# A two-layer decoder trunk on one core: output weights of the last stage split once and kept in DRAM, the scan's carry and the first loads moved to other queues, norm roots as one power, and u kept

## The chip, the cores and the metric

The kernel runs on one core of a Trainium2 chip. The metric is device time in microseconds (us) of one execution, here the median of three runs. Besides the runs one execution was recorded by the hardware profiler; every row of the profile comes from that one.

The engines are named as in the profile: PE is TensorE's matmul, PEld its weight load, DVE VectorE, ACT ScalarE, POOL GpSimd, SP SyncE. SP, ACT and POOL also issue DMAs (SPq, ACTq, POOLq); each of them works through its own queue in order.

## What is computed

x has 2048 rows of 1024. Layer 0 mixes with an mLSTM, layer 1 with an RG-LRU, and a norm ends the trunk:

```python
for layer in range(2):
    u = rmsnorm(x, ln_g[layer])
    y = mlstm_mixer(u, ...) if layer == 0 else rglru_mixer(u, ...)
    x = x + y
return rmsnorm(x, final_g)

def rglru_mixer(u, ...):
    xr, g = split(u @ w_in)                  # 1024 -> 2 x 1536
    xc = causal_dwconv(xr, conv_w, conv_b)   # 4 taps
    r, ig = sigmoid(xc @ w_a + b_a), sigmoid(xc @ w_x + b_x)   # 8 diagonal blocks of 192
    log_a = -8.0 * r * softplus(-lam)
    bt = sqrt(-expm1(2 * log_a)) * (ig * xc)
    h[t] = exp(log_a)[t] * h[t-1] + bt[t]    # scan along the sequence
    return (h * silu(g)) @ w_out             # 1536 -> 1024
```

`rmsnorm` multiplies by the inverse root of the mean square, so each norm needs one root per row of x.

## The kernel before, in words

Activations lie with features on the 128 partitions and time along the free dimension, in blocks of TB = 512 columns, four blocks in all. Each fp32 product is made of three: both operands are split into a high part (a cast, ACT, line 735) and a low part (source minus high part, DVE, line 738), and `mm3` (lines 360 to 364) adds hh, hl and lh in PSUM.

There are four phases, one after the other:

- **a1** (line 385): layer 0's input projections. Two blocks of 512 columns are taken together as the halves of a Strassen-like product (class `Slab`, lines 39 to 286): `u11`, `u21` are parts of the first block's u, `t1` to `t4` and `u22` are combinations of both blocks (`combos`, line 196). It runs for s = 0 and s = 1. `early` (line 230) makes products that need the first block alone while the second block's norm is made (`stat` and `norm`, lines 607 to 611). Weight combinations `s1` to `s4` are split for s = 0, stored to DRAM from POOL's queue (line 90) and loaded by SP for s = 1 (line 95).
- **a2** (line 749): the mLSTM recurrence.
- **b1** (line 1042): layer 0's output projection and layer 1's input projection, the latter again in Strassen-like form.
- **b2** (line 1218): the last stage, that is gates, scan, output projection and the final norm. A step list (lines 1227 to 1234) takes, for each of four blocks, eight gate items ("g", 21 matmuls each) and 24 output items ("r", 12 matmuls each): one g, then three r that belong to five g earlier.

*Norm roots.* `stats_sum` (line 1019) sums squares on PE (`ssum`), DVE scales the sum into `stx` (line 1027), and `rsqrt` (line 334) makes the inverse root `rc` on DVE: a shift, a subtraction and three Newton steps of three, eleven instructions of 128 x 4. Then PE spreads `rc` over the partitions (`rows`, line 140; `srow`, line 1034). It is called twelve times: four times each in a1, b1 and b2.

*u of the first block.* `combos` needs u of the first block in one piece. `backs` (line 187) rebuilds it from high and low parts in eight DVE additions, into tiles of t1 and t4; u of the second block goes to eight tiles `x`, which have eight buffers.

*Weights in b2.* `fetch` (line 1237) brings the next weights; `weights` keeps up to three items ready ahead in high priority. A gate item's raw weights (128 x 896, one buffer) are split in block 0, high and low parts are stored to `d_gw` by POOL (line 1252) and loaded again by SP in blocks 1 to 3 (line 1244), each in one of two buffers. An output item's raw weights (128 x 512, three buffers) are loaded and split in each of the four blocks (lines 1247 and 1249), into one of four buffers.

*First xc.* `load(0, 0)` brings the first three xc tiles by DMAs from ACT's queue (line 1279); all others come from SP's (line 1282).

*Carry.* After each group's three scans (line 1318) POOL copies the last column to `hcarry` (line 1320), which the same group's scan in the next block starts from.

*Order.* The order of instructions in each engine's queue is planned when the kernel is built, from dependences, priorities and planned times; `tc.high_priority()` moves what stands in it ahead.

Of the kernel before, what the change touches and what calls it, by code (L numbers as in the profile page):

```python
# [7 lines left out]
F32 = mybir.dt.float32  # L8
# [30 lines left out]
class Slab:  # L39
# [156 lines left out]
    def combos(self, U, xs, rc, fs, row=None):  # L196
# [7 lines left out]
        us = xs if row is not None else [self.x() for _ in range(KD)]  # L204
# [10 lines left out]
        for j in range(4):  # L215
            U["u22", j] = self.operand("u22", j, us[j + 4], "v")
            v.tensor_tensor(us[j + 4], f2[j], f1[j], op=ALU.subtract)
# [71 lines left out]
class Trunk:  # L289
    def __init__(self, ctx, tc, vecs, gbias):  # L290
# [14 lines left out]
        nc.vector.memset(self.one1, 1.0)  # L305
        self.lc = cp.tile([P, 48], F32, name="lc")
# [27 lines left out]
    def rsqrt(self, pool, out, x, w, rows=P):  # L334
        nc = self.nc
        b = pool.tile([P, w], I32, tag="rsb", name="rsb")
        t = pool.tile([P, w], F32, tag="rst", name="rst")
        nc.vector.tensor_scalar(b[:rows], x.bitcast(I32), 1, None, op0=ALU.logical_shift_right)
        nc.vector.tensor_scalar(out.bitcast(I32), b[:rows], -1.0, float(0x5F3759DF), op0=ALU.mult, op1=ALU.add)
        for _ in range(3):  # L340
            nc.vector.tensor_tensor(t[:rows], out, out, op=ALU.mult)
            nc.vector.scalar_tensor_tensor(t[:rows], t[:rows], -0.5, x, op0=ALU.mult, op1=ALU.mult)
            nc.vector.scalar_tensor_tensor(out, t[:rows], 1.5, out, op0=ALU.add, op1=ALU.mult)

    def stats(self, pool, psp, acc, rc, rb, tag="st"):

        nc = self.nc
        ps = psp.tile([P, 512], F32, tag=tag, name=tag)
        for c in range(4):
            nc.tensor.matmul(ps[:, c:c + 1], acc[:, c * P:(c + 1) * P], self.ones, start=True, stop=True)  # L350
        x = pool.tile([P, 4], F32, tag="stx", name="stx")
        nc.vector.tensor_scalar(x, ps[:, 0:4], 1.0 / DM, EPS, op0=ALU.mult, op1=ALU.add)
        self.rsqrt(pool, rc, x, 4)
        pb = psp.tile([P, 512], F32, tag=tag, name=tag)
        for c in range(4):
            nc.tensor.matmul(pb[:, c * P:(c + 1) * P], rc[:, c:c + 1].to_broadcast([P, P]), self.ident,
                             start=True, stop=True)
        nc.scalar.copy(rb, pb)
# [1139 lines left out]
```

## Time and profile before

| | us |
|---|---|
| median of 3 runs | 3058.34 |
| lowest, highest | 3058.22, 3059.42 |
| profiled execution, its time | 3061.18 |
| profiled execution, its span | 3059.1 |
| mean granted TensorE clock | 0.983 |

The phases lie in the span about as follows: a1 from 0 to 1010 us, a2 to 1710, b1 to 2565, b2 to the end.

| us of the span | PE busy, us | DVE busy | ACT busy | granted clock | DMA share |
|---|---|---|---|---|---|
| 40 to 400 (a1) | 347.9 | 258.1 | 169.6 | 0.98 | 0.67 |
| 1020 to 1700 (a2) | 658.9 | 555.1 | 430.0 | 0.98 | 0.45 |
| 1715 to 2095 (b1) | 372.2 | 235.4 | 114.8 | 1.00 | 0.62 |
| 2340 to 2560 (b1) | 220.0 | 132.1 | 69.0 | 1.00 | 0.62 |
| 2560 to 2600 (b2) | 28.1 | 13.9 | 22.6 | 0.79 | 0.82 |
| 2680 to 2790 (b2) | 105.9 | 86.1 | 78.4 | 0.99 | 0.63 |

A row of a timeline reads: start, duration, engine, line of the kernel, operation, what is written and read, shape, count; in brackets how long the engine had been idle and what ended that. The DMA share is the mean busy share of the core's 16 DMA engines.

### The profile page before, as it was taken

To read this page: it belongs to the slowest core of one execution; us is meant where nothing else is said; L and a number is where in the kernel's file an instruction comes from. 1 tells how busy PE (TensorE), PEld (TensorE's weight loads), DVE (VectorE), ACT (ScalarE), POOL (GpSimd) and SP (SyncE) were. 2 spreads that over 40 slices of the span, in tenths; PEclk is the share of its full clock that TensorE was granted. 3 is DMA by queue.
4 is the path that set the end of the run, shared out by engine and by line. 5 is a ranking of instruction groups with operands and counts; after the bars stand their busy time and mean duration, and the time that the engine had idled before them with its cause. 6 is when DMAs were issued, how large, how long until landed. Compare 5 with 4: busy or idle time off the path is not lost. (4 is left out here: it accounts for less than half of the span.)

```text
span 3059.1 us, 43718 instructions
## 1 busy us (share of the span) xinstructions
PE 2927.9 (96%) x15730; PEld 2506.7 (82%) x15730; DVE 2153.6 (70%) x3774; ACT 1509.3 (49%) x2514; POOL 211.7 (7%) x394
## 2 busy tenths in 40 slices
PE   6999999999999999999999899999999998899997
PEld 4799987899988898989999777877888886687786
DVE  7866789534566688888888555687778374887775
ACT  5444545323344566666666322333445234876772
POOL 0111110000000011111111000000110000110100
PEclk9999999999999999999999999999999998999999
DMA  6766677666777645454443665566666656656643
GB/s 218 255 216 231 230 249 241 204 202 206 222 222 228 193 129 167 128 171 132 148 144 102 200 192 176 182 210 216 217 216 224 206 188 230 240 183 236 237 134 128
DMA packets 308985, 600.63 MB, mean 196 GB/s; under 512 B 27808, under 2 KB 106400, under 8 KB 308768
## 3 DMA queue, kind: packets, MB, share of 16 engines
q1 hardware_dynamic: 222784, 389.79, 41.4%
q10 hardware_dynamic: 59184, 107.77, 10.0%
q0 software_dynamic: 26800, 100.28, 8.5%
q8 instruction: 124, 2.03, 0.3%
q14 instruction: 93, 0.76, 0.1%
HBM read 388.86 MB, written 208.86 MB: 195 GB/s over the span
## 5 line engine op out<-in xcount | busy, mean ns | idle before, releaser
L735 ACT CAST s<-raw 128x512 fp32r<-128x512 f32 (+1 forms) x360 | 222.3, 621 | 497.8 <-PE acc L364 195.4
L738 DVE TENSOR_TENSOR s<-raw,s 128x512 fp32r<-128x512 f32 (+1 forms) x360 | 246.9, 689 | 90.4 <-ACT s L735 84.9
L362 PE MATMUL acc<-yh,s 128*128 128x512 f32 x512 | 202.3, 398 | 10.1 <-ACT yh L735 3.4
L363 PE MATMUL acc<-yl,s 128*128 128x512 f32 x512 | 202.8, 396 | 0.0
L364 PE MATMUL acc<-yh,s 128*128 128x512 f32 x512 | 202.2, 395 | 0.0
L362 PE MATMUL acc<-yh,wh 128*128 128x512 f32 x384 | 150.4, 399 | 14.3 <-ACT yh L735 9.4
L363 PE MATMUL acc<-yl,wh 128*128 128x512 f32 x384 | 153.5, 401 | 0.3 <-DVE yl L738 0.2
L364 PE MATMUL acc<-yh,wl 128*128 128x512 f32 x384 | 152.1, 399 | 1.1 <-DVE wl L738 1.0
L662 DVE SCALAR_TENSOR_TENSOR xc<-xm,vec,xc 128x512 f32<-128x512 f32 x192 | 140.5, 748 | 14.3 <-ACT xc L660 13.4
L735 ACT CAST s<-sum 128x512 fp32r<-128x512 f32 (+1 forms) x120 | 74.3, 620 | 146.4 <-PE pa L364 43.6
L362 PEld LDWEIGHTS acc<-yh,s 128*128 128x128 f32 x512 | 96.6, 189 | 35.5 <-ACT yh L735 3.8
L735 ACT CAST wh<-wr 128x512 fp32r<-128x512 f32 (+1 forms) x104 | 65.4, 641 | 107.8 <-PE acc L363 76.1
L364 PEld LDWEIGHTS acc<-yh,s 128*128 128x128 f32 x512 | 96.8, 189 | 22.7
L363 PEld LDWEIGHTS acc<-yl,s 128*128 128x128 f32 x512 | 96.8, 189 | 22.4 <-DVE yl L738 0.4
L930 DVE SCALAR_TENSOR_TENSOR C<-C,dl,kv 128x516 f32<-128x516 f32 x112 | 83.7, 747 | 44.6 <-PE kv L364 44.5
L738 DVE TENSOR_TENSOR wl<-wr,wh 128x512 fp32r<-128x512 f32 (+1 forms) x104 | 73.5, 717 | 56.2 <-ACT wh L735 50.9
L362 PE MATMUL gate<-xch,wh 128*128 128x512 f32 x224 | 91.9, 411 | 19.2 <-ACT xch L735 9.3
L738 DVE TENSOR_TENSOR s<-sum,s 128x512 fp32r<-128x512 f32 (+1 forms) x120 | 82.6, 689 | 39.3 <-ACT s L735 38.0
L662 DVE SCALAR_TENSOR_TENSOR xc<-xr,vec,xc 128x512 f32<-128x512 f32 x144 | 104.9, 747 | 7.3 <-ACT xc L660 6.3
L735 ACT CAST Ch<-C 128x516 fp32r<-128x516 f32 x120 | 74.8, 623 | 64.9 <-DVE da L948 48.2
L362 PE MATMUL pj<-vwh,xmh 128*128 128x512 f32 x256 | 103.3, 403 | 0.0
L364 PE MATMUL pj<-vwh,xml 128*128 128x512 f32 x256 | 100.4, 392 | 0.0
(418 smaller groups left out, 9615.2 us busy)
## 6 DMA issues: line engine op xcount, KB each, us to landing
d_wx<-s POOLq DMA_DIRECT2D x64, 512.0 KB, 4.0
s<-d_wx SPq DMA_DIRECT2D x64, 512.0 KB, 4.4
raw<-in_wout_dram SPq DMA_DIRECT2D x128, 256.0 KB, 3.1
raw<-in_wxz_dram SPq DMA_DIRECT2D x124, 256.0 KB, 4.4
d_wr<-s POOLq DMA_DIRECT2D x48, 512.0 KB, 3.5
s<-d_wr SPq DMA_DIRECT2D x48, 512.0 KB, 4.6
wr<-in_rwout_dram SPq DMA_DIRECT2D x96, 256.0 KB, 2.9
raw<-in_rwin_dram SPq DMA_DIRECT2D x84, 256.0 KB, 3.9
```

Of the source, the lines that this page charges most:

```text
L362: mm(out, sh, mh, start=first, stop=False, skip_group_check=resumed)
L363: mm(out, sh, ml, start=False, stop=False, skip_group_check=resumed)
L364: mm(out, sl, mh, start=False, stop=last, skip_group_check=resumed)
L662: nc.vector.scalar_tensor_tensor(out, x[:, j:j + TB], self.v(wn, m * 4 + j), out, op0=ALU.mult, op1=ALU.add)
L735: a = nc.scalar.copy(hi, src)
L738: b = (nc.gpsimd if lo_eng == "p" else nc.vector).tensor_tensor(lo, src, hi.bitcast(F32), op=ALU.subtract)
L930: nc.vector.scalar_tensor_tensor(C2, C2, self.dl[:, r:r + 1], p2, op0=ALU.mult, op1=ALU.add)
```

## The change

- `rsqrt` becomes one POOL instruction, a power with exponents from a tile of -0.5, in all twelve places.
- In a1 `combos` gets `held`: `backs` is not called; the scaled x tiles of the first block are passed as u, and u of the second block goes to tiles of t1 and t4.
- In b2 high and low parts lie side by side in one tile `both`. Output weights are split in block 0 alone, stored by POOL to a new DRAM tile `ow`, and loaded by SP in blocks 1 to 3 in one DMA of 512 KB. Gate weights are stored and loaded in one DMA in place of two.
- The first three xc are loaded from POOL's queue.
- The carry is copied by ACT.
- `stats`, which nothing calls, is gone.

```diff
-    def combos(self, U, xs, rc, fs, row=None):
+    def combos(self, U, xs, rc, fs, row=None, held=False):
...
-        us = xs if row is not None else [self.x() for _ in range(KD)]
+        if held:
+            us = [self.temp("t4", "l", j) for j in range(4)] + [self.temp("t1", "h", j) for j in range(4)]
+        else:
+            us = xs if row is not None else [self.x() for _ in range(KD)]
...
             U["u22", j] = self.operand("u22", j, us[j + 4], "v")
+            if held:
+                us[j + 4] = f2[j]
             v.tensor_tensor(us[j + 4], f2[j], f1[j], op=ALU.subtract)
...
+        self.mhalf = cp.tile([P, 4], F32, name="mhalf")
+        nc.vector.memset(self.mhalf, -0.5)
...
-    def rsqrt(self, pool, out, x, w, rows=P):
-        nc = self.nc
-        b = pool.tile([P, w], I32, tag="rsb", name="rsb")
-        t = pool.tile([P, w], F32, tag="rst", name="rst")
-        nc.vector.tensor_scalar(b[:rows], x.bitcast(I32), 1, None, op0=ALU.logical_shift_right)
-        nc.vector.tensor_scalar(out.bitcast(I32), b[:rows], -1.0, float(0x5F3759DF), op0=ALU.mult, op1=ALU.add)
-        for _ in range(3):
-            nc.vector.tensor_tensor(t[:rows], out, out, op=ALU.mult)
-            nc.vector.scalar_tensor_tensor(t[:rows], t[:rows], -0.5, x, op0=ALU.mult, op1=ALU.mult)
-            nc.vector.scalar_tensor_tensor(out, t[:rows], 1.5, out, op0=ALU.add, op1=ALU.mult)
...
+    def rsqrt(self, out, x, w):
+        self.nc.gpsimd.tensor_tensor(out, x, self.mhalf[:, 0:w], op=ALU.pow)
...
-                    t[:] = [S.invrms(acc1), S.backs(U)]
+                    t[:] = [S.invrms(acc1), (xs[0:4], xs[4:8])]
...
-                    S.combos(U, x1, *t)
+                    S.combos(U, x1, *t, held=True)
...
-                wh = wp.tile([P, m], F32R, tag="wh" + kind, name="wh", bufs=2 if kind == "g" else 4)
-                wl = wp.tile([P, m], F32R, tag="wl" + kind, name="wl", bufs=2 if kind == "g" else 4)
-                if kind == "g" and b > 0:
-                    for j, t in enumerate((wh, wl)):
-                        nc.sync.dma_start(t.bitcast(F32), D["gw"][i, j])
+                both = wp.tile([P, 2 * m], F32R, tag="w" + kind, name="w" + kind, bufs=2 if kind == "g" else 4)
+                wh, wl = both[:, 0:m], both[:, m:2 * m]
+                keep = D["gw" if kind == "g" else "ow"][i]
+                if b > 0:
+                    nc.sync.dma_start(both.bitcast(F32), keep)
                     return wh, wl
                 raw = wp.tile([P, m], F32, tag="wr" + kind, name="wr", bufs=1 if kind == "g" else 3)
...
                 self.split_into(wh, wl, raw, "a", "v")
-                if kind == "g":
-                    for j, t in enumerate((wh, wl)):
-                        nc.gpsimd.dma_start(D["gw"][i, j], t.bitcast(F32))
+                nc.gpsimd.dma_start(keep, both.bitcast(F32))
                 return wh, wl
...
-                        nc.scalar.dma_start(c[:, t], src[t])
+                        nc.gpsimd.dma_start(c[:, t], src[t])
...
-                nc.gpsimd.tensor_copy(hc[:, p * 3:p * 3 + 3], xc[:, :, TB - 1])
+                nc.scalar.copy(hc[:, p * 3:p * 3 + 3], xc[:, :, TB - 1])
...
-                         ("gw", [8, 2, P, 896])):
+                         ("gw", [8, P, 1792]), ("ow", [24, P, 1024])):
```

More of the change, by code (lines that the diff above doesn't have):

```diff
@@ L332, in v @@
         return self.vec[:, o:o + 1]
-    def rsqrt(self, pool, out, x, w, rows=P):
-        nc = self.nc
-        b = pool.tile([P, w], I32, tag="rsb", name="rsb")
-        t = pool.tile([P, w], F32, tag="rst", name="rst")
-        nc.vector.tensor_scalar(b[:rows], x.bitcast(I32), 1, None, op0=ALU.logical_shift_right)
-        nc.vector.tensor_scalar(out.bitcast(I32), b[:rows], -1.0, float(0x5F3759DF), op0=ALU.mult, op1=ALU.add)
-        for _ in range(3):
-            nc.vector.tensor_tensor(t[:rows], out, out, op=ALU.mult)
-            nc.vector.scalar_tensor_tensor(t[:rows], t[:rows], -0.5, x, op0=ALU.mult, op1=ALU.mult)
[L343 to L358, printed above, removed]
+    def rsqrt(self, out, x, w):
+        self.nc.gpsimd.tensor_tensor(out, x, self.mhalf[:, 0:w], op=ALU.pow)
     def mm3(self, out, sh, sl, mh, ml, first, last, resumed=False):
@@ L1027, in stats_sum @@
         nc.vector.tensor_scalar(x, ps[:, 0:4], 1.0 / DM, EPS, op0=ALU.mult, op1=ALU.add)
-        self.rsqrt(pool, rc, x, 4)
+        self.rsqrt(rc, x, 4)
     def stats_rows(self, psp, rc, tag):
```

## The prediction

> **What bounds the kernel now.** I read the page first, then PE's idle stretches in the timeline, then what DVE, ACT, POOL and SP did in those stretches. Where a row of the timeline ends in a bracket, the engine was idle for that many us before it, until the named instruction of the named engine was done.
>
> ```profile
> span 3059.1 us, 43718 instructions
> PE 2927.9 (96%) x15730; PEld 2506.7 (82%) x15730; DVE 2153.6 (70%) x3774; ACT 1509.3 (49%) x2514; POOL 211.7 (7%) x394
> ```
>
> PE is busy for 2927.9 of 3059.1 us, so all idle time of PE is 131 us, and the change takes no matmul away. What it can give lies in those 131 us and in what the clock loses after them. So I listed PE's gaps and asked which of them end on something that the change touches. These do:
>
> ```profile
> 19.75 2.05 PE L140 MATMUL rows<-ident,rc 128*128 128x128 f32 x8 [4.46 <-DVE rc L343]
> 55.38 2.07 PE L140 MATMUL rows<-ident,rc 128*128 128x128 f32 x8 [5.66 <-DVE rc L343]
> ...
> 532.03 0.50 PE L362 MATMUL pd<-u22h,s 128*128 128x512 f32 x1 [0.80 <-DVE z L253]
> ...
> 1910.44 1.13 PE L140 MATMUL rows<-ident,rc 128*128 128x128 f32 x8 [1.09 <-DVE rc L343]
> ...
> 2102.55 0.79 PE L362 MATMUL pa<-u21h,s 128*128 128x512 f32 x1 [5.61 <-ACT p L263]
> ...
> 2570.41 0.80 PE L362 MATMUL gate<-xch,wh 128*128 128x512 f32 x1 [5.36 <-ACT xch L735]
> 2579.77 0.80 PE L362 MATMUL gate<-xch,wh 128*128 128x512 f32 x1 [3.96 <-ACT xch L735]
> ...
> 2786.45 1.74 PE L362 MATMUL acc<-yh,wh 128*128 128x512 f32 x4 [4.11 <-ACT yh L735]
> 2898.59 1.34 PE L362 MATMUL acc<-yh,wh 128*128 128x512 f32 x4 [4.08 <-ACT yh L735]
> 2997.19 0.51 PE L362 MATMUL acc<-yh,wh 128*128 128x512 f32 x1 [1.05 <-ACT wh L735]
> ...
> 3048.17 2.08 PE L1034 MATMUL srow<-ident,rc 128*128 128x128 f32 x8 [2.43 <-DVE rc L343]
> ```
>
> Four wait for the root of a norm, two for the first xc, two for y at a block's end in the last stage, one for weights; those at 532 and 2102 end in a stretch where DVE does work that the change takes away. A long gap costs more than itself, for the granted clock is low behind it (the PEclk column, before the DMA share):
>
> ```profile
> 55.00:60.00 5.00, 4.62 (x16) 4.06 (x17) 2.83 (x6) 0.62 (x1) 0.00 (x0) 0.54 0.59 198
> 2560.00:2626.00 66.00, 46.52 (x166) 34.64 (x164) 33.62 (x31) 43.53 (x54) 10.83 (x18) 0.87 0.81 284
> 2640.00:2745.00 105.00, 102.86 (x442) 83.02 (x441) 86.98 (x81) 82.31 (x103) 11.54 (x4) 0.98 0.59 202
> 2786.00:2792.00 6.00, 5.55 (x17) 4.42 (x18) 4.22 (x3) 5.35 (x6) 0.00 (x0) 0.72 0.95 342
> 2790.00:2900.00 110.00, 105.92 (x469) 86.82 (x469) 85.83 (x95) 77.15 (x101) 10.95 (x4) 1.00 0.62 213
> ```
>
> 0.54 over 5 us is 2.3 us lost, 0.72 over 6 us is 1.7.
>
> **The norm roots.** Eleven small DVE instructions after `stx` become one POOL instruction, twelve times.
>
> ```profile
> 41.76 0.15 DVE L1027 TENSOR_SCALAR stx<-ssum 128x4 f32<-128x4 f32 x1
> ...
> 49.57 0.68 DVE L185 TENSOR_TENSOR temp<-u21h,u21l 128x512 f32<-128x512 f32 x1
> ...
> 52.53 0.69 DVE L117 TENSOR_TENSOR sum<-sum,raw 128x512 f32<-128x512 f32 x1 [1.01 <-DMA raw<-in_wxz_dram]
> ...
> 55.17 0.15 DVE L343 SCALAR_TENSOR_TENSOR rc<-rst,rc 128x4 f32<-128x4 f32 x1
> L1320 POOL COPY hcarry<-xc 128x3 f32<-128x3 f32 x16 | 40.3, 2520 | 336.2 <-DVE xc L1318 336.2
> L967 POOL TENSOR_TENSOR frs<-frs,mh 128x2 f32<-128x2 f32 x32 | 23.3, 728 | 0.0
> L969 POOL TENSOR_TENSOR frs<-frs 128x2 f32<-128x2 f32 x32 | 6.2, 195 | 2.5
> ```
>
> The second root is not slow by its arithmetic: it takes 13.4 us (41.76 to 55.32) because full tiles of DVE work lie between its eleven steps. One instruction cannot be interleaved. Its price: a power of two columns takes 728 ns, a product of the same shape 195. If the difference is fixed, four columns take about 0.73 us; if it goes by the column, 0.195 + 4 x 0.267 = 1.26. Both are estimates. In the last norm nothing else runs: the 2.43 us gap becomes 0.15 for `stx`, 0.73 to 1.26, and two handovers of about 0.1, so 1.1 to 1.6. Gain 0.8 to 1.3, I take **1.0**.
>
> In the first two norms POOL has company. The copy of three columns takes 2520 ns, far more than the power, so something holds it. The copies stand beside DVE products from two SBUF tiles (`g`, `xcl`); the powers of phase a2 that I looked at stand beside a `vl` that reads PSUM. The Trainium skill's page "GPSIMD Engine Reference", section 8 "Key points", says that POOL shares its SBUF interfaces with VectorE and that DVE instructions with two SBUF inputs contend with it; the trace agrees with its 2520 ns. In the first two norms DVE runs splits and sums of two SBUF tiles almost without a pause, so a root may be held there as the copies are. POOL's queue also holds the stores of kept weights: the root can stand behind one that waits for a split. In the first norm the price is between the tail's (gain 3) and a root held for about 2 us behind three splits (gain 1); I take **2**. In the second, removing eight `backs` (0.6 us apart, some 4.8 us) and eleven steps empties DVE, so even a held root should be there before PE asks for it at 49.7 (55.38 less 5.66). Then 5.66 and most of 2.3 of clock go, 8.0 at best. But a few gaps follow until 78 that end on t2 and t3, which DVE makes after the root; they stay. If the root is held until the pause of 1.01 us before 52.53, rc comes at about 53.3 for 55.32, and only 2 go. I take **6.5**.
>
> The third wait, at 1910, meets an empty POOL queue and goes: **1.1**. At 532 PE waits for DVE while DVE does the second half's `backs`; they go: **0.8** (0 to 2, since the sum of the remaining work can also shift). `held` keeps u in its eight x tiles and puts the new terms in t1 and t4, which `backs` held before; the next user of x is a load several groups later, so I cost it at nothing. If a t4 tile came free late, t1 and t4 would wait, not t2 and t3.
>
> At about 2102 DVE is again the last to finish, with eight interleaved steps in its queue of 0.07 to 0.2 us each. I take **0.7**, 0 to 1.5.
>
> **First xc and the start of the last stage.**
>
> ```profile
> 2565.83 0.33 ACTq L1279 DMA_DIRECT2D xc<-d_xr  x1
> 2569.76 0.33 ACTq L1279 DMA_DIRECT2D xc<-d_xr  x1
> 2566.74 0.54 POOL L1172 DMA_DIRECT2D d_g<-g  x1 [2.27 <-ACT g L1170]
> 2573.79 7.24 DMA wr<-in_rgate_dram
> ...
> 2615.08 8.01 DMA wr<-in_rgate_dram
> SPq L1311 <- DMA d_g<-g: 17.1, 1, 17.1
> ```
>
> On ACT the third xc is issued 3.9 us after the first, behind a cast that waits for the first. On POOL the three go out 0.54 apart, unless the last store of g, which waits for ACT, stands ahead of them: the first then starts at about 2567.3, 1.5 us later than now. So the 3.96 us gap may go and the 5.36 may grow by 1.5. But neither sets the pace: the chain of waits runs here through six loads of gate weights in one buffer, from 2573.79 to 2623, because SP's queue is held by the load of g, which waits for that same store. PE is ahead of it, and what it saves at xc it waits for at the next gate weights. So 0 from the move. Against it: the first four output weights are now stored too, 4 x 0.5 MB on the software queue. Its row below gives 100.28 MB in 8.5% of 3059 us, 386 GB/s, so 5.4 us more for DMA engines that are at 0.81 over 66 us. The six loads take about 6.4 us each; slower by 5 to 10% they cost 2 to 4. I take **-2** (from +3, if the third xc helps after all, to -6).
>
> **Output weights kept.** In blocks 1 to 3 there are 72 splits less:
>
> ```profile
> L735 ACT CAST wh<-wr 128x512 fp32r<-128x512 f32 (+1 forms) x104 | 65.4, 641 | 107.8 <-PE acc L363 76.1
> L738 DVE TENSOR_TENSOR wl<-wr,wh 128x512 fp32r<-128x512 f32 (+1 forms) x104 | 73.5, 717 | 56.2 <-ACT wh L735 50.9
> q0 software_dynamic: 26800, 100.28, 8.5%
> 2765.99 0.62 ACT L735 CAST wh<-wr 128x512 fp32r<-128x512 f32 x1 [4.37 <-PE acc L363]
> 2766.69 5.11 ACTq L1390 DMA_DIRECT2D out_dram<-x  x3
> 2771.84 0.62 ACT L735 CAST wh<-wr 128x512 fp32r<-128x512 f32 x1 [5.23 <-DMA out_dram<-x]
> 2772.36 1.26 ACT L1307 ACTIVATE ig<-gate,lc 128x512 f32<-128x512 f32 x2
> ```
>
> Their busy time, 46 us of ACT and 52 of DVE, is not the gain, for neither engine is the bound. The gain is in what the casts hold up. ACT takes its queue in order: it stood idle for 76.1 us before casts that waited for PE to free a weight buffer, and at 2766 to 2772 two such casts kept the last two `ig` of the block waiting, although their gates were done. From `ig` the work goes on through three scans and g to `yh`, for which PE waits 4.11 us at 2786. Without the casts `ig` follows the eight output stores at about 2767, some 5 us earlier; that is more than the gap. So 4.11 + 1.7 goes, and the same again at 2898. The five small gaps from 2997 to 3007, 3.0 us, wait for these splits themselves. At best 5.8 + 5.8 + 3.0 = 14.6.
>
> The price is that SP now waits where ACT did. A weight tile is one of four, so its load can start when PE is through with the fourth item before it, and it must have landed three products and one gate later. With 469 matmuls in 105.92 us (0.226 each) that is 57 x 0.226 = 12.9 us. What a load of this kind takes:
>
> ```profile
> s<-d_wx SPq DMA_DIRECT2D x64, 512.0 KB, 4.4
> SPq L1247 <- DVE wl L738: 217.2, 85, 5.7
> ```
>
> 4.4 us, and SP's longest hold for a weight buffer is 5.7: 10.1 in all, inside 12.9. The gate weights are already loaded this way and no PE gap ends on one of their loads. Bytes per block rise by 24 x 0.25 MB = 6.3 MB. At 213 GB/s for a share of 0.62, a full share moves 344 GB/s, so that is 18 us: from 0.62 of 110 us to 0.79, a share that the start of the stage already runs at. Where x and the output stores crowd at the block's end I allow 1 to 2 us three times, together -4. I take **+10.5** (0 to 14.6). In block 0 the splits stay and 20 stores are added, 10.5 MB or 27 us: 0.59 becomes 0.85 of 105 us. The raw loads run three buffers ahead; I take **-2** (0 to -5).
>
> The carry's copy leaves POOL, where nothing waited for it; on ACT it stands before the cast of g, which comes after the same scan. Its next reader is a block away. Nothing; between 16 x 0.15 us of ACT (the small `stx` row) and the 40.3 us that POOL took, on an engine that is busy for 77 of 110 us and loses 15 to the change.
>
> Sum: 2 + 6.5 + 0.8 + 1.1 + 0.7 - 2 + 10.5 - 2 + 1.0 = 18.6 us gained. The profiled execution took 3061.2 us, its span 3059.1; the median of the runs is 3058.3. I apply the sum to the median: **3040 us** (3058.3 - 18.6 = 3039.7).
>
> **Rivals.** *The root starves on POOL.* The root is held for a whole run of DVE splits, as the copies are. Then the first norm gives 1 and the second 2, as worked out above: 18.6 - 1 - 4.5 = 13.1 us in all, 3045. For it are the 2520 ns; against it that DVE has less to do and stops by itself once PE wants the root. This is what the skill's rule on shared interfaces would make of the change. Chance 0.17.
>
> *y is not what was late.* If the block ends find another brake (the output stores on ACT, DVE's xc split, a late x1), the 10.5 becomes 1 to 2: 3049. Against it: no other instruction stands between 2766 and 2772 on ACT. Chance 0.18.
>
> *Kept loads come too late: slower.* If hold and transfer together pass 12.9 us, PE waits at each step of blocks 1 to 3. It takes 2.8 us more than the worst pair above. At 1.2 us over in each of the 24 steps it costs 29 us and the 10.5 is lost: 3058.3 - 8.1 + 29 = 3079. For it is a DMA share of 0.79 with SP in strict order behind waits for PE; against it the gate loads. Break-even is 0.34 us per step. Chance 0.10.
>
> *It does little.* The order in the queues is planned when the kernel is built, from planned times; with other instructions it shifts everywhere, and new gaps of 1 to 5 us, as at 2102, take back what is won. 3052 to 3064, chance 0.13.
>
> That leaves 0.42 for the forecast, 3030 to 3044. A measurement tells about 0.2%, 6.1 us, from no change. The first three cases lie below 3052.2 but for a little of the second rival: faster 0.74. Same 0.15, slower 0.11. The range from 3028 to 3056 leaves out the slow rival, part of the case that it does little, and the corner where all bounds are best (about 3023).
>
> **What would show it.** Right: the waits for rc at 20, 55 and 1910 gone or under 2 us; no gap over 1 us before acc at two of the block ends, with `ig` right behind the output stores; a last wait of 1.1 to 1.6 us; 72 casts and 72 `wl` fewer. Wrong: acc in blocks 1 to 3 waiting for a DMA into the kept tiles; gate loads at the stage's start well above 6.4 us; a POOL power of several us with rows waiting for it.

## The result and the profile after

The changed kernel takes 3045.18 us (median of four runs, 3043.84 to 3045.92) against 3058.88 for the kernel before (3058.22 to 3065.80): a ratio of 0.9947, interval 0.9935 to 0.9960. 13.7 us are gained, where 18.6 were forecast. The profiled execution took 3045.92 us. The head of its page (span; busy time, share and instructions by engine):

```profile
span 3044.1 us, 43340 instructions
PE 2921.0 (96%) x15730; PEld 2503.5 (82%) x15730; DVE 2083.8 (68%) x3555; ACT 1470.6 (48%) x2458; POOL 195.4 (6%) x409
```

DVE lost 70 us of work and ACT 39, POOL 16; the span lost 15.0. Here are the waits of PE in the timeline of the changed kernel that answer to those listed for the kernel before (start, duration, then in brackets the idle time and who ended it). The times lie 2 to 20 us earlier than there, for what is gained and lost adds up along the way.

```profile
17.43 2.07 PE L140 MATMUL rows<-ident,rc 128*128 128x128 f32 x8 [1.74 <-POOL rc L343]
45.06 1.05 PE L140 MATMUL rows<-ident,rc 128*128 128x128 f32 x8
...
65.61 0.50 PE L347 MATMUL pc<-t3h,s 128*128 128x512 f32 x1 [2.44 <-ACT t3h L720]
...
1895.77 1.16 PE L140 MATMUL rows<-ident,rc 128*128 128x128 f32 x8 [0.56 <-POOL rc L343]
...
2089.94 0.50 PE L347 MATMUL pa<-u21h,s 128*128 128x512 f32 x1 [3.98 <-ACT p L269]
...
2559.02 0.79 PE L347 MATMUL gate<-xch,wg 128*128 128x512 f32 x1 [7.69 <-ACT xch L720]
2572.06 0.79 PE L347 MATMUL gate<-xch,wg 128*128 128x512 f32 x1 [6.36 <-ACT wg L720]
...
2771.21 1.20 PE L347 MATMUL acc<-yh,wr 128*128 128x512 f32 x4 [1.12 <-ACT yh L720]
2878.25 1.19 PE L347 MATMUL acc<-yh,wr 128*128 128x512 f32 x4 [0.38 <-ACT yh L720]
2983.70 0.76 PE L347 MATMUL acc<-yh,wr 128*128 128x512 f32 x1 [7.70 <-DMA wr<-d_ow]
...
3032.96 2.08 PE L1019 MATMUL srow<-ident,rc 128*128 128x128 f32 x8 [1.41 <-POOL rc L343]
```

The wait of the second norm is gone (no bracket at 45.06), and two block ends that waited 4.11 and 4.08 us now wait 1.12 and 0.38. Three waits have grown: the first gate, 5.36 to 7.69; the next one in that stage, 3.96 for an xc before and 6.36 for gate weights now; and the same place in block 3, where PE had 1.05 as its longest wait and now has 7.70.

A ledger puts this together. The program is cut where PE starts the first matmul of a kind, named by the tile that it writes (`s` is the first product of scores in a2, a block of the last stage ends where its sum of squares starts, and the last stage itself begins where PE ends b1). The length of each piece is compared with the terms of the forecast:

| Piece (us) | before | after | gained | forecast |
|---|---|---|---|---|
| start to first `pa` (first norm) | 23.3 | 21.0 | 2.3 | 2 |
| to first `oa` (second norm in it) | 137.6 | 131.3 | 6.3 | 6.5 |
| to a2's first `s` | 863.9 | 862.7 | 1.2 | 0.8 |
| a2 from there | 688.1 | 685.0 | 3.0 | 0 |
| b1 | 852.3 | 851.3 | 1.0 | 1.8 |
| last stage, to the end of block 0 | 178.5 | 181.8 | -3.2 | -4 |
| block 1 | 112.3 | 107.8 | 4.5 | blocks 1 to 3 together 10.5 |
| block 2 | 112.2 | 107.0 | 5.1 | |
| block 3 | 74.6 | 79.6 | -4.9 | |
| tail | 16.4 | 16.7 | -0.3 | 1.0 |

The 3.0 us of a2 are no part of the change: nothing was edited there, and the runs below, whose a2 is the same, have 685.4 to 688.5. One large term is wrong: block 3, which lost 5 us.

The power by itself, in the table of groups (line, engine, operation, count, busy us, mean ns, idle before), beside the carry's copies on ACT:

```profile
L343 POOL TENSOR_TENSOR rc<-stx,mhalf 128x4 f32<-128x4 f32 x12 | 14.7, 1223 | 697.6 <-DVE stx L1012 696.0 <-DVE hist L1141 1.7
L1303 ACT COPY hcarry<-xc 128x3 f32<-128x3 f32 x16 | 3.1, 195 | 83.0 <-DVE xc L1301 83.0
```

Single powers, from POOL's timeline, at the second norm and at the end:

```profile
40.51 1.39 POOL L343 TENSOR_TENSOR rc<-stx,mhalf 128x4 f32<-128x4 f32 x1 [23.13 <-DVE stx L1012]
...
3031.90 1.01 POOL L343 TENSOR_TENSOR rc<-stx,mhalf 128x4 f32<-128x4 f32 x1 [80.71 <-DVE stx L1012]
```

1.01 us where DVE is idle, 1.39 beside its work on two SBUF tiles, never more than 1.48 in this kernel: the root is not starved. So the rival that had it held for a whole run of splits falls. The Trainium skill's page "GPSIMD Engine Reference", section 8, says that POOL contends with such DVE instructions; the trace agrees in kind, with 0.4 us here and far more at the copies (below).

Why does block 3 wait? The bracket of the 7.70 names a load into a kept weight tile. But ACT's timeline ends on the same instant:

```profile
2962.98 0.59 ACT L1370 COPY rb<-srow 128x512 f32<-128x512 f32 x1 [2.09 <-PE srow L1019]
2964.38 5.63 ACTq L1373 DMA_DIRECT2D out_dram<-x  x8
2970.04 1.28 ACT L1290 ACT_TABLE_LOAD   x1 [6.48 <-DMA out_dram<-x]
2971.34 1.84 ACT L1290 ACTIVATE ig<-gate,lc 128x512 f32<-128x512 f32 x3
...
2982.26 1.47 ACT L720 CAST yh<-g 128x1536 fp32r<-128x1536 f32 x1 [1.60 <-DVE g L1304]
```

The cast of `yh` ends at 2983.73, PE goes on at 2983.70. SP's timeline has the load (the first of eight that the row groups):

```profile
2976.15 29.54 SPq L1229 DMA_DIRECT2D wr<-d_ow  x8
```

In the trace this load lands 7.4 us after its issue, at 2983.6 (loads into these tiles take 3.5 to 7.6 us in this stretch). So load and y end within 0.2 us of each other, and either could be what PE waits for.

### The profile page after: what moved, and what is told of

Read it like the earlier page. It is cut to its first block, busy times and chain, and to the rows that moved or that the text cites. A ratio compares the mean times of both kernels' runs of the same rounds, so it can differ in the third digit from the quotient of the medians.

```text
span 3044.1 us, 43340 instructions
## 1 busy us (share of the span) xinstructions
PE 2921.0 (96%) x15730; PEld 2503.5 (82%) x15730; DVE 2083.8 (68%) x3555; ACT 1470.6 (48%) x2458; POOL 195.4 (6%) x409
## 5 line engine op out<-in xcount | busy, mean ns | idle before, releaser
L347 PE MATMUL acc<-yh,wr 128*128 128x512 f32 x384 | 149.3, 397 | 15.1 <-DMA wr<-d_ow 7.7
L348 PE MATMUL acc<-yl,wr 128*128 128x512 f32 x384 | 151.2, 394 | 0.0
L349 PE MATMUL acc<-yh,wr 128*128 128x512 f32 x384 | 150.8, 393 | 0.0
L647 DVE SCALAR_TENSOR_TENSOR xc<-xm,vec,xc 128x512 f32<-128x512 f32 x192 | 140.3, 747 | 14.5 <-ACT xc L645 12.5
L348 PEld LDWEIGHTS acc<-yl,s 128*128 128x128 f32 x512 | 97.2, 190 | 23.2 <-DVE yl L723 1.0
L347 PE MATMUL gate<-xch,wg 128*128 128x512 f32 x224 | 92.7, 417 | 21.5 <-ACT wg L720 11.7
L347 PEld LDWEIGHTS acc<-yh,wr 128*128 128x128 f32 x384 | 72.7, 190 | 34.1 <-issue 8.1
L348 PE MATMUL pj<-vwl,xmh 128*128 128x512 f32 x256 | 100.0, 391 | 0.0
```

Source lines behind the costliest of these rows:

```text
L347: mm(out, sh, mh, start=first, stop=False, skip_group_check=resumed)
L348: mm(out, sh, ml, start=False, stop=False, skip_group_check=resumed)
L349: mm(out, sl, mh, start=False, stop=last, skip_group_check=resumed)
L647: nc.vector.scalar_tensor_tensor(out, x[:, j:j + TB], self.v(wn, m * 4 + j), out, op0=ALU.mult, op1=ALU.add)
```

## The experiments

The single times of one kernel scatter by several us (the kernel before had 3055.85 to 3068.15 beside the first four), so the verdicts rest on the lengths of pieces in the traces, with the medians beside them. The kernel before had medians of 3061.78, 3062.65 and 3062.84 beside the three groups of four. Pieces that an edit leaves alone scatter too: in the kernels that have both the power and u kept, the piece with the second norm takes 130.3 to 132.7 us, and b1, wherever the root is a power, 851.3 to 854.3.

**Output weights split in each block again.**

```diff
-                if b > 0:
+                if b > 0 and kind == "g":
...
-                nc.gpsimd.dma_start(keep, both.bitcast(F32))
+                if kind == "g":
+                    nc.gpsimd.dma_start(keep, both.bitcast(F32))
```

> The changed kernel, but its output weights are split again in each of the four blocks (no stores to ow, no kept loads); gate weights stay kept as changed. My theory: the casts on ACT made the waits for yh at the ends of blocks 1 and 2, and the kept loads make the one wait of 7.7 us for a load in block 3. So both gaps of about 4 us come back (blocks 1 and 2 each some 5 us longer), the 7.7 us wait goes (block 3 some 5 us shorter), block 0 gains up to 2 us without the stores: 3046 to 3049 us. Rival: the carry on ACT and the roots off DVE made the blocks shorter, not the casts; then the gaps stay away and the time is 3036 to 3040.

Measured: 3046.34 us, ratio 0.9956 (0.9942 to 0.9970), as good as with kept weights. Last stage to the end of block 0: 178.4; blocks 112.9, 111.5, 74.7. So keeping them gains 5.1 and 4.5 in blocks 1 and 2, and loses 3.4 and 4.9 in blocks 0 and 3: 1.4 us in all, next to nothing. The theory held, but for block 0, which gave more than the 2 us allowed. At the end of block 1 a cast stands on ACT ahead of the last two `ig` again:

```profile
2757.18 0.62 ACT L720 CAST wr<-wr 128x512 fp32r<-128x512 f32 x1 [5.82 <-DMA out_dram<-x]
2757.71 1.26 ACT L1291 ACTIVATE ig<-gate,lc 128x512 f32<-128x512 f32 x2
```

In block 3 of this kernel PE waits only for splits, as before the change; first and last of five such rows of the timeline:

```profile
2981.64 0.50 PE L347 MATMUL acc<-yh,wr 128*128 128x512 f32 x1 [0.94 <-ACT wr L720]
...
2990.92 0.50 PE L347 MATMUL acc<-yh,wr 128*128 128x512 f32 x1 [0.75 <-ACT wr L720]
```

**Kept output weights loaded from POOL's queue.**

```diff
-                    nc.sync.dma_start(both.bitcast(F32), keep)
+                    (nc.gpsimd if kind == "r" else nc.sync).dma_start(both.bitcast(F32), keep)
```

> The changed kernel, but the kept output weights of blocks 1 to 3 are loaded from the POOL queue in place of the SP queue. My theory: in block 3 the loads stand behind x loads in the SP queue that wait for output stores, while the last steps have no gate product to cover them; from POOL the 7.7 us wait falls below 3 us and the time is 3037 to 3041 us. Rival: the DMA engines are full there (up to 440 GB/s), the load lasts 7.5 us whatever queue it comes from; the wait stays at 6 us or more and the time at 3044 to 3047.

Measured: 3046.34 us, ratio 0.9951 (0.9938 to 0.9963); block 3 79.3 us, so nothing is gained. PE's wait in its timeline, the load in POOL's, and the cast in ACT's:

```profile
2985.61 0.76 PE L347 MATMUL acc<-yh,wr 128*128 128x512 f32 x1 [7.24 <-DMA wr<-d_ow]
```

```profile
2978.67 0.54 POOL L1229 DMA_DIRECT2D wr<-d_ow  x1 [2.21 <-PE acc L349]
```

```profile
2984.62 1.48 ACT L720 CAST yh<-g 128x1536 fp32r<-128x1536 f32 x1 [1.60 <-DVE g L1304]
```

PE starts at 2985.61, half a us before `yh` is ready at 2986.10, so its first matmul there does not need that y: the bracket is right, it waits for a load. And the load isn't late because of its queue. Its own bracket says that it waited for PE: the tile came free when PE was done with the item that it runs just before. In the order of PE's queue, seven matmuls of an item of the second half stand at this place, ahead of items whose weights are loaded before it. There are four tiles, so its load can only go out when the last item before it is through, and PE stands for the whole transfer, 6.9 us here. In seven further traces with this order (the changed kernel and six of the runs) it is 7.1 to 7.7 us from the load's issue to PE's start, while the end of `yh` lies between 0.1 us after and 0.4 us before that start. So two limits meet here: with the weights in time, PE would have run those seven matmuls (1.6 us at 0.226) and then waited for y. By an estimate from the changed kernel's rows, some 6 of the 7.7 us would have stayed: PE runs dry at 2976.0 and y ends at 2983.7. The rival's numbers came; that full DMA engines make the transfer so long was not tried.

**Roots on DVE in eleven steps again**, u still kept.

```diff
-        self.nc.gpsimd.tensor_tensor(out, x, self.mhalf[:, 0:w], op=ALU.pow)
+        (the shift, the subtraction and three Newton steps of the kernel before)
```

> The changed kernel, but the norm roots are made by the eleven DVE instructions again. My theory: the root's eleven steps between full tiles of DVE work made most of the gain in the first norms; without it rows waits again: about 2 us at the first norm, 3 to 6 at the second, 1 in the projection stage: 3049 to 3054 us. Rival: leaving out backs made that gain (DVE had time), the root itself was not late; then only the first norm and the tail count, 2 to 3 us: 3046 to 3048.

Measured: 3052.99 us, ratio 0.9972 (0.9963 to 0.9981). Rows from PE's timeline, at the second norm and at the wait of b1:

```profile
48.83 1.16 PE L140 MATMUL rows<-ident,rc 128*128 128x128 f32 x8
...
67.58 0.51 PE L356 MATMUL pc<-t3h,s 128*128 128x512 f32 x1 [3.11 <-ACT t3h L729]
...
2094.62 0.80 PE L356 MATMUL pa<-u21h,s 128*128 128x512 f32 x1 [5.60 <-ACT p L269]
```

The power costs or gains nothing at the second norm: without it there is no wait either (no bracket at 48.83), and the piece takes 130.2 us against 131.3. So the time lies in the theory's range, but its largest term did not come. The power gains 2.0 at the first norm (23.0 to 21.0) and 1.0 in the last wait (2.43 to 1.41). b1 is 4.3 us longer here (855.6 against 851.3), but up to 3 us of that is scatter; its two waits that the power shortens account for 2.1 (1.07 to 0.56, 5.60 to 3.98).

**First xc from ACT's queue again.**

```diff
-                        nc.gpsimd.dma_start(c[:, t], src[t])
+                        nc.scalar.dma_start(c[:, t], src[t])
```

> The changed kernel, but the first three xc tiles are loaded from ACT's queue as before. My theory: the pace there is set by the chain of gate weights, so it makes no difference: 3044 to 3047 us. Rival: on POOL the third xc stands behind a store of output weights that waits for their split, and costs PE; from ACT it is 2 to 4 us faster, 3041 to 3043.

Measured: 3049.94 us, ratio 0.9962 (0.9950 to 0.9975). PE's first gate waits 5.3 us and not 7.7, but the last stage takes 181.7 us to the end of block 0 as against 181.8: what is saved at the first wait is given back. The median lies 5 us above the changed kernel's, the profiled span 1.2; no piece shows the difference.

**Output stores of blocks 0 to 2 from POOL's queue.**

```diff
-                    (nc.scalar if m % 2 or not last else nc.sync).dma_start(outT[m, :, bs], x2[m])
+                    (nc.gpsimd if not last else nc.scalar if m % 2 else nc.sync).dma_start(outT[m, :, bs], x2[m])
```

> The changed kernel with one edit: the output stores of blocks 0 to 2 are issued on POOL and not on ACT. Theory (the last block's wait of 7.70 us before acc is a wait for yh, and yh is late because the last three ig stand on ACT behind eight output stores that each wait for a DVE product): ig runs at once after the rb copy, some 5 us earlier; the eight DVE products still stand ahead of the scans, so some 4 us of it arrive: the gap falls to 3 to 4.5, the last block from 79.6 to 75 to 77 us, the time to about 3041. Rival (the order in which PE's matmuls were planned leaves it nothing else to do at that place, and the chain from rb through the DVE products to yh is long by itself): the gap stays between 6 and 8 and the last block between 78 and 80, the time within 1.5 us of 3045. If the stores on POOL cost anything, it shows at the ends of blocks 0 to 2.

Measured: 3044.41 us, ratio 0.9946 (0.9933 to 0.9958); block 3 75.2 us, blocks 1 and 2 107.8 each. ACT's timeline at the same place, then PE's and DVE's:

```profile
2967.69 0.59 ACT L1370 COPY rb<-srow 128x512 f32<-128x512 f32 x1 [2.07 <-PE srow L1019]
...
2969.59 0.69 ACT L1290 ACTIVATE ig<-gate,lc 128x512 f32<-128x512 f32 x1
...
2972.51 0.69 ACT L1290 ACTIVATE ig<-gate,lc 128x512 f32<-128x512 f32 x1 [0.68 <-PE gate L349]
...
2982.66 1.47 ACT L720 CAST yh<-g 128x1536 fp32r<-128x1536 f32 x1 [1.60 <-DVE g L1304]
```

```profile
2984.19 1.37 PE L347 MATMUL acc<-yh,wr 128*128 128x512 f32 x4 [3.48 <-ACT yh L720]
```

```profile
2968.31 5.39 DVE L1372 SCALAR_TENSOR_TENSOR x<-x,vec,rb 128x512 f32<-128x512 f32 x8 [0.89 <-ACT rb L1370]
2973.62 1.75 DVE L1297 SCALAR_TENSOR_TENSOR xc<-ig,xc 128x1536 f32<-128x1536 f32 x1
```

From rb to the end of `yh` it takes 16.4 us instead of 20.8, as the theory of the stores has it, and the wait is 3.48 instead of 7.70, of the size expected. But the edit also changed the planned order: the item of the second half no longer stands ahead of the three that need y, so the wait for the load is gone as well. Both had to go for the wait to fall; that y comes earlier is the edit's, that the load is out of the way is the order's. The profiled span gained only 1.5, because a2 took 688.4 us in this run.

**Backs at the second norm again, power kept.**

```diff
-                    t[:] = [S.invrms(acc1), (xs[0:4], xs[4:8])]
+                    t[:] = [S.invrms(acc1), S.backs(U)]
...
-                    S.combos(U, x1, *t, held=True)
+                    S.combos(U, x1, *t)
```

> The changed kernel with one part undone: the eight backs stand between the second norm's statistics and its sums again and the new terms go to x tiles, while the root stays a power on POOL. Theory (the run with the roots on DVE and without backs had no wait at the second norm, so it was the backs that ended it, not the power): rows of the second norm waits again, 2 to 5 us, and the stretch from the first pa to the first oa of the second half grows from 131.3 us to 133.5 to 137; about 3 to 5 us in all, 3049. Rival (either alone is enough, since one instruction on another engine isn't held by what DVE does): no wait, 131 to 132 us, the time within 1.5 us of 3045.

Measured: 3063.52 us, ratio 1.0001 (0.9992 to 1.0010): the whole gain of the change is gone. The piece with the second norm takes 148.3 us; 133.5 to 137 were expected, so the direction was right and the size was not. It isn't the rows that wait. From PE's timeline, and DVE's:

```profile
45.35 1.05 PE L140 MATMUL rows<-ident,rc 128*128 128x128 f32 x8
...
54.49 0.80 PE L349 MATMUL pa<-u11h,s 128*128 128x512 f32 x1 [4.37 <-DVE s L723]
...
66.33 0.50 PE L347 MATMUL pb<-t2h,s 128*128 128x512 f32 x1 [1.75 <-ACT t2h L720]
```

```profile
48.96 0.69 DVE L185 TENSOR_TENSOR temp<-u11h,u11l 128x512 f32<-128x512 f32 x1
51.94 0.69 DVE L117 TENSOR_TENSOR sum<-sum,raw 128x512 f32<-128x512 f32 x1 [2.30 <-DMA raw<-in_wxz_dram]
```

The root is there at 42.2, but in DVE's queue the products and sums of the second block stand behind the eight `backs`, the last of them behind a weight sum that waits 2.30 us for its DMA, and in the planned order only 59 `pa` matmuls stand between `ssum` and the first `pb` (81 in the changed kernel); the other 22 come at 96. PE runs dry, and between 40 and 100 it is idle for 14.4 us and not 4.1, at a granted clock of 0.67 to 0.82 in the four stretches of 10 us from 50 to 90, where the changed kernel has 0.83 to 1.00. All four combinations have now been run, and the length of this piece in us is:

| | backs | u kept |
|---|---|---|
| eleven steps on DVE | 137.6 | 130.2 |
| power on POOL | 148.3 | 131.3 |

Keeping u gains 7.4 with the old root and 17.0 with the new one. The power by itself would have lost 10.7 here, in the planned order that came with it; how much of that is the order's was not tried.

**First four output weights not stored in block 0** but split again and stored in block 1.

```diff
+                late = kind == "r" and i < 4
-                if b > 0:
+                if b > (1 if late else 0):
...
+                if b or not late:
```

> The changed kernel with one edit: the first four output weights are not stored in block 0 but split from the raw weights again and stored in block 1. Theory (those four stores, on the DMA engines and on POOL's queue while the gate weights load, are what made the start of the last stage 3.2 us longer): the stretch from the last stage's start to the end of block 0 falls from 181.8 to 178.5 to 179.5 us, block 1 grows by up to 1 us; the time 3043. Rival (it is the other 20 stores of block 0, which take part of the bandwidth, or the changed order): 181 to 182 us, the time as it was, 3045 to 3046.

Measured: 3042.32 us, ratio 0.9945 (0.9931 to 0.9958); 178.9 us to the end of block 0, block 1 108.1. The number came as the theory had it, the mechanism did not. If the stores held up the gate weights, the sixth gate item should start earlier. Counted from the start of the last stage, it starts at 54.6 us here, 53.4 in the changed kernel, 48.9 in the kernel before. The gain comes later: from the sixth gate item to the end of block 0 it takes 124.3 us, and 128.4 in the changed kernel. That figure goes with the order in which PE's matmuls were planned: four of the kernels here (this one, the one with splits, and two below) have whole gate items ahead of whole output items after 2606 and take 123.6 to 124.3; those that mix them there take 128 to 132. The order alone is not enough: the next run has whole items too and takes 139, with new waits. And no run changed the order by itself, so that it is the cause is not shown.

**Two raw buffers for gate weights** (and two, for three, for the raw output weights).

```diff
-                raw = wp.tile([P, m], F32, tag="wr" + kind, name="wr", bufs=1 if kind == "g" else 3)
+                raw = wp.tile([P, m], F32, tag="wr" + kind, name="wr", bufs=2)
```

> The changed kernel with two raw buffers for the gate weights and two, for three, for the raw output weights. Theory (one raw buffer makes each gate weight's load wait for the cast and the difference of the one before it, and this chain sets the pace until 2606): loads overlap with the splits, the waits of 6.36, 3.08 and 1.36 before the gate matmuls lose 3 to 6 us in all, and the stretch to the end of block 0 falls from 181.8 to 176 to 179 us; the time about 3041. Rival (DMA bandwidth sets that pace, or the split's place in ACT's and DVE's order): loads only take longer, 181 to 182 us; with two raw buffers for output weights the later part of block 0 could gain waits of its own and the time rise by 1 to 3.

Measured: 3056.06 us, ratio 0.9982 (0.9973 to 0.9990), 11 us slower than the changed kernel. To the end of block 0 it takes 189.4 us. The longest new wait, in PE's timeline:

```profile
2597.05 2.07 PE L347 MATMUL gate<-xch,wg 128*128 128x512 f32 x4 [8.74 <-ACT xch L720]
```

The third gate item does start at 23.2 us and not at 30.2, but then PE waits for an xc, and the sixth starts at 50.6, 2.8 earlier. After it 13.7 us of waits follow in block 0 (7.0 in the changed kernel). So with two raw buffers the gate weights do come earlier, and the wait moves to xc and y. The rival's part came as well: from the third on, the loads of gate weights take 8.9 to 12.1 us from issue to landing (3.8 to 8.3 for the same six in the changed kernel). Whether the loss comes from the second buffer or from the raw output weight tile that paid for it was not tried.

**Both edits that shortened a piece** (stores on POOL, first four stored later).

> Both edits that shortened a stage, together: output stores of blocks 0 to 2 issued on POOL, and the first four output weights stored in block 1 instead of block 0. If each acts in its own stage, the stretch from the last stage's start to the end of block 0 takes 179 us (181.8 in the changed kernel) and the last block 75 to 75.5 (79.6), blocks 1 and 2 107 to 108.5 each: 7 us below the changed kernel, about 3038. Rival (the planned order shifts with each edit, and the two gains are of the order that each happened to get): one of the two stages falls back to its old length, 3041 to 3043.

Measured: 3042.13 us, ratio 0.9938 (0.9925 to 0.9951). To the end of block 0 178.2, block 3 76.1, its wait again 3.5: each acts in its own piece. The time still lies 4 us above the 3038 expected. Block 1 had 112.6 us in this profiled run and 108.2 in the next.

**The same with the first xc from ACT's queue.**

> As the kernel with both edits, and the first xc loaded from ACT's queue again instead of POOL's. Theory (the chain of gate weights through one raw buffer sets the pace, so an earlier or later xc is worth nothing in either place): the stretch to the end of block 0 stays at 178.5 to 179.5 us and the time within 1 us of the kernel with both edits. Rival (without the early stores the chain is short enough for the first xc to count, and its first wait is 7.5 us on POOL's queue against 5.3 on ACT's): 176 to 178 us, 1 to 3 us faster.

Measured: 3042.55 us, ratio 0.9939 (0.9927 to 0.9951): no difference in the time. Inside, both theories fall. The sixth gate item starts at 49.8 us, as early as in the kernel before, and yet block 0 ends at 182.2: PE has the mixed order again and waits 9.1 us after that item. So either edit, xc on POOL (54.1 to 55.9 in the four kernels without early stores) or the early stores (52.7 with xc on ACT), goes with a delay of the sixth gate item by 3 to 6 us, and both together (53.4) delay it no more. Whether block 0 ends 178 to 180 or 181 to 182 us after the start goes, in the kernels with the change, with the planned order, not with that delay.

**The final norm's rows three steps later**, on top of both edits.

```diff
+                for _ in range(0 if last else 3):
+                    yield
                 rb = self.stats_rows(pm, rc, "mm")
```

> As the kernel with both edits, and three more steps before the final norm's rows of blocks 0 to 2, so that the eight DVE products of the finished block stand behind the scans and yl of the block that runs and no longer ahead of them. Theory (what is left of the last block's wait, 3.48 us, is these eight products, 5.39 us, between ig and the first scan): the wait falls below 1 us and the last block from 75.2 to between 71.5 and 73; the ends of blocks 1 and 2, without a wait already, stay within 0.5 us; the time about 3035. Rival (another link of that chain, ig itself or the last gates, comes as late, or the products now hold the sums at the next half's end): the last block stays between 74 and 76, or blocks 1 to 3 get waits of 1 to 3 us at the ends of halves; 3037 to 3040.

Measured: 3040.39 us, ratio 0.9935 (0.9922 to 0.9947), the lowest median of all. PE's timeline at the end of the first half in block 2 and at the place of the wait in block 3, and ACT's at the latter:

```profile
2890.97 0.50 PE L347 MATMUL acc<-yh,wr 128*128 128x512 f32 x1 [1.76 <-DVE x L1348]
...
2980.43 1.23 PE L347 MATMUL acc<-yh,wr 128*128 128x512 f32 x4 [2.20 <-ACT yh L720]
```

```profile
2978.91 1.47 ACT L720 CAST yh<-g 128x1536 fp32r<-128x1536 f32 x1 [1.60 <-DVE g L1306]
2980.28 0.58 ACT L1374 COPY rb<-srow 128x512 f32<-128x512 f32 x1
```

The eight products now stand behind `yl`, and the wait falls from 3.5 to 2.2, not below 1, and the time lies 5 us above the 3035 expected: `ig` waits for its gates, and from there two DVE products, three scans and a product of 1.76 us still stand before the cast. Block 3 took 75.6, block 2 109.4 with a new wait for x: the rival's picture. Between this kernel and the one with both edits nothing is settled; their intervals overlap.

**Carry's copy on POOL again.**

```diff
-                nc.scalar.copy(hc[:, p * 3:p * 3 + 3], xc[:, :, TB - 1])
+                nc.gpsimd.tensor_copy(hc[:, p * 3:p * 3 + 3], xc[:, :, TB - 1])
```

> The changed kernel with one part undone: the carry's copy is on POOL again. Theory (its reader is a block away, so nothing waits for it on either engine): every stage within 0.5 us of the changed kernel apart from the clock's scatter, 3045 plus or minus 1.5, although each copy takes about 2.5 us on POOL and 0.19 on ACT. Rival (on ACT it stands between the scan and the cast of g, on POOL it competes with DVE's scans and products for SBUF): a difference of 0.2 us per group of gates, 1 to 3 us in the last stage, in the one direction or the other.

Measured: 3047.98 us, ratio 0.9957 (0.9944 to 0.9971). From the start of the last stage to the end of block 3 it takes 476.7 us, 476.2 in the changed kernel. The median lies 2.8 us above the changed kernel's, outside the 1.5 allowed; the profiled span is 4.0 longer, and a2 and b1, which the edit leaves alone, are 2.1 and 3.0 longer in it. The group of copies, then one of them with DVE's timeline beside it:

```profile
L1303 POOL COPY hcarry<-xc 128x3 f32<-128x3 f32 x16 | 35.7, 2232 | 256.0 <-DVE xc L1301 256.0
```

```profile
2714.01 1.71 POOL L1303 COPY hcarry<-xc 128x3 f32<-128x3 f32 x1 [2.85 <-DVE xc L1301]
```

```profile
2713.92 1.76 DVE L1304 TENSOR_TENSOR g<-xc,g 128x1536 f32<-128x1536 f32 x1
```

2232 ns against 195 on ACT, and nobody waits for it: worth nothing on either engine. Each of the 16 copies ends 0.05 us after a DVE instruction with two inputs in SBUF, 15 times this product and once a `yl`, so that a copy lasts as long as DVE's work beside it, 0.9 to 6.2 us. That is the contention of the Trainium skill's page "GPSIMD Engine Reference", section 8 "Key points"; the trace agrees, with a large number here.

## Why the prediction was right and where it failed

The sign, the range and most terms held. The forecast lies 5 us below the time that was measured, and one term, block 3, is more than that off; the ratio's interval, 12 to 20 us gained, still contains the 18.6. The pieces up to the last stage, without a2, gained 10.8 us where 11.1 were forecast. The largest term, kept output weights, came to about 1.4 us with all that it costs. That the time fell into the range all the same is in part the width of the range: with nothing for kept weights the sum would have been 12.1, or 3046.

- **First norm, 2:** 2.3. **Tail, 1.0:** the wait fell by 1.0 as worked out; the piece did not get shorter in the profiled run, because its 24 small matmuls were busy for 5.18 us and not 4.17, at a granted clock of 0.55 and not 0.61. In the other runs with the power the tail took 14.7 to 16.4 us.
- **Price of the power:** neither estimate was right. With DVE idle it takes 1.01, between 0.73 and 1.26; the mean of 1.223 is near the upper one only because DVE holds some of the twelve up.
- **Second norm, 6.5:** 6.3, and the t3 waits stayed as foretold. But the step took `backs` and steps together as what empties DVE. The run with the old root shows that `backs` alone did it, and the run with `backs` that a root which is ready early gives nothing while the sums stand behind `backs`.
- **The wait at 532, 0.8:** the number came, the mechanism did not. The `backs` are gone, but PE still waits 0.63 us at this place for DVE's `z`; the piece gained 1.2, within the scatter of the runs (860.5 to 863.2).
- **b1, 1.1 + 0.7:** the two waits lost 0.5 and 1.6, near the terms; the piece gained 1.0 only, less than its scatter.
- **Start of the last stage and block 0, -4:** -3.2. The size was right, its reason is not shown. "What it saves at xc it waits for at the next gate weights" was confirmed. That the early stores slow the six loads of gate weights was not: from issue to landing they take 6.2 us in the mean, 6.4 in the kernel before. And without those stores the sixth gate item came no earlier with xc on POOL (54.6 against 53.4), though 2.9 us earlier with xc on ACT (49.8 against 52.7).
- **Blocks 1 and 2, 5.8 each:** 4.5 and 5.1. The mechanism was right: with the casts back both blocks take 112.9 and 111.5.
- **Block 3, +3.0, less 1 to 2 of the allowance:** -4.9. It shows one of the prediction's own signs of being wrong, acc waiting for a DMA into a kept tile. The step that failed is the reach of the kept loads: "its load can start when PE is through with the fourth item before it, and it must have landed three products and one gate later". That gives 12.9 us only if PE takes the items in the order of the loads. At the one place where no gate matmuls are left to run, PE's order puts an item of the second half forward, and its load has no time at all: it goes out when PE has just run dry. The price of the load itself held: it landed 7.6 us after PE's last matmul, inside the 10.1 that were allowed for hold and transfer and inside the 12.9; but no part of the 12.9 was there. In the kernel before, 34 matmuls of the second half stand ahead of the first that needs the last `yh`, with splits in each block 31, in the changed kernel 7; raw weights in three buffers ahead of the four tiles had made that possible (read from the queues; more buffers were not tried). The five waits of 3.0 us for splits did go, and a wait of 7.70 took their place. Behind it stands a second one that the prediction had not seen either: at this block end all eight output stores stand ahead of all three `ig` on ACT, so that y is no earlier than the load. By the estimate above, this second limit alone would have kept some 6 of the 7.7 us.
- **The rivals:** "y is not what was late" named the output stores on ACT as the other brake, and that is what holds y in block 3. "Kept loads come too late" was priced as 1.2 us in each of 24 steps; it came as 7.7 us in one. SP's view of waits from 2960 to 2990 has one hold for a weight tile in these 30 us (us in total, times, longest):

```profile
SPq L1229 <- PE acc L349: 2.4, 1, 2.4
```

  It is another load's; the late one goes out 0.15 us after PE's last matmul. So SP's hold was not what failed. The longest in the whole span, 14.5 us, ends at 2991: that is the load after the late one, which stands while PE stands. "The root starves" had 3045, the time that was measured, but its mechanism did not come: the first two norms gained 2.3 and 6.3 where it had 1 and 2. "It does little" did not come either: what was won early stayed won.

## What to carry to other kernels

A wait that goes because its cause is removed exposes the next thing in the same queue; before counting it, look at what will then stand first in that queue, and how many matmuls are left to cover it. Two edits at one place must be priced as a table of four: here the power alone would have lost 10.7 us, kept u alone won 7.4, and both together won 6.3. When two candidates for a wait end within 0.2 us, one trace can't tell them apart; a few variants of the kernel, in which the two shift against each other, can.

## What had not been expected of the hardware

A power of 128 x 4 on POOL takes 1.01 to 1.04 us with DVE idle. When a DVE instruction with two inputs in SBUF is under way as it starts, it ends 0.86 to 0.90 us after that instruction, in every trace with the power: it takes 1.38 to 1.48 us beside sums and splits of 0.7 us, and 2.55 beside the product `g`, as in the run with the first four stores later (POOL's and DVE's timelines):

```profile
2734.54 2.55 POOL L343 TENSOR_TENSOR rc<-stx,mhalf 128x4 f32<-128x4 f32 x1 [11.38 <-DVE stx L1012]
```

```profile
2734.44 1.76 DVE L1306 TENSOR_TENSOR g<-xc,g 128x1536 f32<-128x1536 f32 x1
```

Beside a sum with one input in PSUM (`x` from `acc`) it takes 1.03. So what the root can lose is set by the length of the one DVE instruction that it meets. The copies of 128 x 3 are held in the same way, 2.23 us in the mean where ACT needs 0.195; why some of them sit through several DVE instructions, and a power through one only, is open.

A load of 512 KB into a kept tile lands 3.5 to 7.6 us after its issue in block 3 of the changed kernel (2958 to 2984), where output stores and x1 loads run beside it.
